# Input projection in wide channel groups with two half sums, and the first norm's squares from channel-major x

## The chip, the core and the metric

The kernel runs on one core of one Trainium2 chip. The metric is device time in microseconds (us): the median of three runs is 1089.92 us (1089.47 to 1090.38). The trace below comes from one more execution, taken with the hardware profiler.

## The reference, cut to what matters

One streaming-encoder layer, 256 tokens, model width 2048, everything in float32:

```
h = rmsnorm(x, norm_mix_g)                 # x is 256 x 2048
a, g, q, k, v = split(h @ w_in)            # 1024 columns each
u = a * sigmoid(g); u = causal_dwconv(u, 31 taps) + b
u = layernorm(u over 1024 channels); conv_out = silu(u)
o = diff_attention(q, k, v, lam)           # 8 heads, 2 x 64 each
mix = concat(conv_out, rmsnorm(o)) @ w_out;  x = x + mix
gate, up = split(rmsnorm(x, norm_ffn_g) @ w_up)    # 2 x 5632
x = x + (gelu(causal_dwconv(gate, 3 taps)) * up) @ w_down
return rmsnorm(x, norm_final_g)
```

## The kernel before, in words

Every large product is built from split operands: a float32 number is held as a high part (rounded to the matmul's type) plus a low part (the rest). Three partial products are summed: high weight x high activation, high weight x low activation, low weight x high activation. Activations live transposed in `xT` (channels on partitions, then chunk k of 128 channels, then high and low side by side, 256 tokens each). Weights stream from memory in pieces of 1 MB (`raw`) over SyncE's queue; ScalarE casts a half piece to `hi` (L151) and VectorE subtracts to get `lo` (L152). One such pair holds four k of a 256-column group. In this document that is a **chunk**. `hi` and `lo` have three buffers each, so the casts can run at most that far ahead of TensorE.

Stages in TensorE's order:

1. While the first weights arrive, 20 small warm-up products (L240) and then the first group of a and of g, k by k (L283). x arrives channel-major (`xt`, two first pieces through ScalarE's queue) and is scaled and split (L113, L114) as it comes. All four accumulator banks of the pool `acc` are in use here.
2. From here TensorE's order is written out by hand (`manual_schedule`). `channel_group` (L202 to L213) computes 256 output channels as two banks, with three matmuls of 256 columns per k and bank (L208, L209, L210). It is called for the groups a1, g1, a2, g2, a3, g3; then `v_slab` computes half of v token-major; then q0, k0, q1, k1, q2, k2, a quarter of v, q3, k3, and the last quarter of v. After each chunk `tick` issues one background step (scores, transposes, values or store of an attention head pair, a step of the layer norm) and two taps of the 31-tap convolution.
3. Layer norm over channels, w_out, then the FFN. The FFN's w_up uses `wide_group` (L179): one matmul of 512 columns with the high weights over the high and the low activations side by side (L187), and one of 256 columns with the low weights (L190), adding into the second half of the bank. The two half sums are added by `halves` (ScalarE copies one half out, VectorE adds the other, L234). w_down is token-major (L218 to L220).
4. The final norm and eight stores.

The norm's factor is applied after the projection: `rb1` holds 1/rms of every token, spread over all partitions, and each a, g and k result is multiplied by it (L375, L383, L531). To get it, x is also loaded token-major in four pieces (`x_sb`), squared and summed on ScalarE (L295), reduced on VectorE (L298), raised to -1/2 on GpSimd (L95, L96), made into two diagonal matrices on VectorE (L102), spread by TensorE (L103) and copied out (L104). The first a and g results are copied out of their banks beforehand (L374, L382), so the banks come free without `rb1`.

On every engine but TensorE a list scheduler sets the order at build time by priority; `prio` shifts a step's priority. A convolution tap is either one VectorE instruction per 128 channels (L350), or ScalarE products (L345) followed by one VectorE add (L346). Scores come out of TensorE, then VectorE adds the mask (L431), ScalarE takes the exponential (L435), VectorE combines the two softmaxes (L445).

Of the kernel before, what the change touches and what calls it, by code (L numbers as in the profile page):

```python
# [27 lines left out]
def block_kernel(  # L28
# [97 lines left out]
    XPARTS = [1, 1, 1, 1, 2, 2, 2, 2, 2, 2]  # L126
    WARM = 10
    SIDE = 2
# [50 lines left out]
    def wide_group(w, c0, xT):  # L179
        ps = [acc.tile([P, 2, T], F32, name="acc") for _ in range(2)]  # L180
        for kc in range(0, KD, 8):
            for k, hi, lo in load(w, kc, 8, c0, GW):
# [17 lines left out]
        return ps  # L200

    def channel_group(w, c0, xT, n_conv=0, ready=None):  # L202
        ps = [acc.tile([P, T], F32, name="acc") for _ in range(2)]
        for kc in range(0, KD, 8):
            for k, hi, lo in ready[kc : kc + 8] if ready else load(w, kc, 8, c0, GW):
                for n in range(2):
                    cs = slice(n * P, (n + 1) * P)
                    nc.tensor.matmul(ps[n], lhsT=hi[:, cs], rhs=xT[:, k, 0, :], start=(k == 0), stop=False)  # L208
                    nc.tensor.matmul(ps[n], lhsT=hi[:, cs], rhs=xT[:, k, 1, :], start=False, stop=False)  # L209
                    nc.tensor.matmul(ps[n], lhsT=lo[:, cs], rhs=xT[:, k, 0, :], start=False, stop=(k == KD - 1))  # L210
                if k % 4 == 3:
                    tick(n_conv)
        return ps  # L213
# [18 lines left out]
    def halves(dst, ps, pool):  # L232
        t1 = pool.tile([P, T], F32, name="half")
        nc.scalar.copy(t1, ps[:, 1, :])  # L234
        nc.vector.tensor_tensor(dst, ps[:, 0, :], t1, op=ALU.add)

    with ph1:
# [5 lines left out]
        ss1 = const.tile([P, NT, D // XW], F32, name="ss1")  # L243
# [10 lines left out]
        for i, nk in enumerate(XPARTS):  # L254
            raw = wraw[k0 * 2 // KD][:, k0 % (KD // 2) : k0 % (KD // 2) + nk, :]
            spans = [(0, GW), (CC, GW)]
            if i < SIDE:
                nc.scalar.dma_start(xraw[:, k0 : k0 + nk, :], xt[:, k0 : k0 + nk, :])
            pieces.append((k0, nk, raw, spans))
            k0 += nk  # L260
        nc.scalar.activation(const.tile([P, 8], F32, name="touch"), mhalf, AF.Copy)
        for i, (k0, nk, raw, spans) in enumerate(pieces):
            if i == 0:
                fetch(mix_g, norm_mix)
# [22 lines left out]
        early = load(wi, 0, 8, GW, GW)  # L287
        for i in range(D // XW):
            if i == 2:
                early.extend(load(wi, 8, 4, GW, GW))  # L290
            cs = slice(i * XW, (i + 1) * XW)
# [4 lines left out]
        early.extend(load(wi, 12, 4, GW, GW))  # L296
# [4 lines left out]
        load_params()  # L301
        with prio(300):
# [64 lines left out]
        for j in range(NP):  # L367
            pa = first[:2] if j == 0 else channel_group(wi, j * GW, xT, n_conv=RATE_A, ready=early if j == 1 else None)
# [8 lines left out]
            pg = first[2:] if j == 0 else channel_group(wi, CC + j * GW, xT, n_conv=RATE_A)  # L377
            for n in range(2):
                g_ = p2.tile([P, T], F32, name="g_")
                if j == 0:  # L380
                    with prio(ATT):
                        nc.vector.tensor_copy(g_, pg[n])  # L382
                nc.vector.tensor_tensor(g_, g_ if j == 0 else pg[n], rb1, op=ALU.mult)  # L383
# [137 lines left out]
        for j in range(H // 2):  # L521
            pq = channel_group(wi, 2 * CC + j * GW, xT, n_conv=RATE_Q)
            qT, kT = [], []
            for n in range(2):
                q_ = p2.tile([P, T], F32, name=f"q{n}")
                nc.scalar.copy(q_, pq[n])
                qT.append(q_)
            pk = channel_group(wi, 2 * CC + H * P + j * GW, xT, n_conv=RATE_Q)
# [76 lines left out]
        bg.extend([seq(ln_total, ln_mean, turn), value, None, ln_var, put, ln_apply])  # L605
# [50 lines left out]
    with ExitStack() as ph2:  # L656
# [10 lines left out]
        for j in range(DFF // GW):  # L667
            pg = wide_group(wu, j * GW, h2T)
            ge = []
            for n in range(2):  # L670
                f = 2 * j + n
                gp = gps[f % 4]
                halves(gp[:, FP:], pg[n], q2)
# [15 lines left out]
            for n in range(2):  # L689
                f = 2 * j + n  # L690
                us = q2.tile([P, T], F32, name="us")
                halves(us, pu[n], q2)
# [12 lines left out]
        STORES = (("dve", 0, 512), ("act", 512, 1024), ("dve", 1024, 1536), ("dve", 1536, 2048))  # L705
# [9 lines left out]
        def finish(t, ss):  # L715
# [4 lines left out]
            c0 = D - XW  # L720
            for eng, lo_, hi_ in STORES:
                xs = x_sb[:, t, lo_:hi_]
                if hi_ == D:
                    nc.vector.scalar_tensor_tensor(xs, xs, r3, gf[:, c0:], op0=ALU.mult, op1=ALU.mult)
                elif eng == "act":
# [119 lines left out]
```

## Time and profile before

| | |
|---|---|
| median of 3 runs | 1089.92 us (1089.47 to 1090.38) |
| the profiled execution's own time | 1090.31 us |
| its span in the trace | 1088.5 us |
| TensorE busy | 1077.5 us (99%) |
| VectorE busy | 764.9 us (70%) |
| ScalarE busy | 599.1 us (55%) |
| GpSimd busy | 15.3 us (1%) |
| DMA | 205.89 MB, mean 189 GB/s |

The busy shares are means over stages that differ: VectorE is busy in nine tenths or more of the slices that hold the convolution and in five to seven tenths later. TensorE's matmuls overlap in the trace (each is shown with its whole duration), so the distance from start to start is the cost of one, not its shown duration. The same holds, by less, on VectorE.

### The profile page before, as it was taken

How to read it: one execution, taken by the hardware profiler on the slowest of the kernel's cores; microseconds unless marked ns; L12 is line 12 of the kernel's file. 1: busy time of each engine (PE TensorE's matmuls, PEld its weight loads, DVE VectorE, ACT ScalarE, POOL GpSimd, SP SyncE). 2: the span in 40 equal slices, each digit the busy share in tenths (PEclk: the TensorE clock that was granted, in tenths of full speed). 3: DMA queues.
4: the chain of work that ended last, by engine and by line, in shares of the span. 5: the costliest groups of instructions: out<-in, count | busy, mean ns of one | idle time of the engine just before them, and what ended most of it. 6: DMA issues, size and time to landing. Idle time of an engine off the chain costs nothing.

```text
span 1088.5 us, 16124 instructions
## 1 busy us (share of the span) xinstructions
PE 1077.5 (99%) x6311; PEld 951.5 (87%) x6311; DVE 764.9 (70%) x1202; ACT 599.1 (55%) x973; POOL 15.3 (1%) x44
## 2 busy tenths in 40 slices
PE   9999999999999999999999999999999999999996
PEld 9999999998888888888888888888888888888885
DVE  6799999988765777776777677776777445454544
ACT  6776889886755454545445444544545434343432
POOL 0000000001000000000000000000000000000000
PEclk9999999999999999999999999999999999999998
DMA  9755544444555555555555555555555655555553
GB/s 352 244 192 185 190 165 152 155 163 148 201 178 178 186 194 192 184 183 181 193 191 193 194 187 180 184 189 189 194 193 190 231 192 196 192 194 193 195 166 107
DMA packets 32844, 205.89 MB, mean 189 GB/s; under 512 B 3712, under 2 KB 4480, under 8 KB 9600
## 3 DMA queue, kind: packets, MB, share of 16 engines
q1 hardware_dynamic: 32336, 203.55, 54.2%
q8 instruction: 49, 0.80, 0.3%
q0 software_dynamic: 144, 1.05, 0.2%
q10 hardware_dynamic: 288, 0.26, 0.1%
q14 instruction: 27, 0.22, 0.1%
HBM read 202.75 MB, written 2.10 MB: 188 GB/s over the span
## 4 chain that ended last, share of the span: by engine, by line
PE 97%; DMA 1%; DVE 1%; ACT 0%; issue 0%; POOL 0%; POOLq 0%; DVEq 0%; SPq 0%; ACTq 0%
PE acc L187 30%; PE acc L190 15%; PE acc L218 11%; PE acc L220 11%; PE acc L219 11%; PE acc L208 5%; PE acc L210 5%; PE acc L209 5%; PE acc L283 2%; DMA v_sb<-in_w_in 1%; PE misc L629 0%; PE misc L426 0%; PE misc L423 0%; PE misc L454 0%; DVE lo L152 0%; ACT hi L151 0%
## 5 line engine op out<-in xcount | busy, mean ns | idle before, releaser
L152 DVE TENSOR_TENSOR lo<-raw,hi 128x1024 fp32r<-128x1024 f32 x368 | 450.0, 1223 | 270.0 <-ACT hi L151 268.7
L151 ACT CAST hi<-raw 128x1024 fp32r<-128x1024 f32 x368 | 386.6, 1051 | 389.3 <-PE acc L220 171.5
L187 PE MATMUL acc<-actT,hi 128*128 128x512 f32 x1408 | 481.7, 395 | 0.0
L190 PE MATMUL acc<-actT,lo 128*128 128x256 f32 x1408 | 368.8, 280 | 0.0
L187 PEld LDWEIGHTS acc<-actT,hi 128*128 128x128 f32 x1408 | 253.3, 188 | 48.5
L190 PEld LDWEIGHTS acc<-actT,lo 128*128 128x128 f32 x1408 | 265.4, 188 | 13.7
L219 PE MATMUL acc<-lo,fT 128*128 128x512 f32 (+1 forms) x355 | 137.5, 387 | 0.0
L220 PE MATMUL acc<-hi,fT 128*128 128x512 f32 (+1 forms) x355 | 137.5, 387 | 0.0
L208 PE MATMUL acc<-actT,hi 128*128 128x256 f32 x448 | 127.6, 285 | 0.0
L210 PE MATMUL acc<-actT,lo 128*128 128x256 f32 x448 | 127.0, 283 | 0.2 <-DVE lo L152 0.2
L209 PE MATMUL acc<-actT,hi 128*128 128x256 f32 x448 | 126.8, 283 | 0.0
L218 PE MATMUL acc<-hi,fT 128*128 128x512 f32 (+1 forms) x355 | 123.8, 387 | 0.0
L208 PEld LDWEIGHTS acc<-actT,hi 128*128 128x128 f32 x448 | 85.9, 192 | 0.7 <-issue 0.7
L210 PEld LDWEIGHTS acc<-actT,lo 128*128 128x128 f32 x448 | 85.9, 192 | 0.4 <-DVE lo L152 0.4
L209 PEld LDWEIGHTS acc<-actT,hi 128*128 128x128 f32 x448 | 85.9, 192 | 0.0
L220 PEld LDWEIGHTS acc<-hi,fT 128*128 128x128 f32 x355 | 66.7, 188 | 13.7
L219 PEld LDWEIGHTS acc<-lo,fT 128*128 128x128 f32 x355 | 66.7, 188 | 13.6
L218 PEld LDWEIGHTS acc<-hi,fT 128*128 128x128 f32 x355 | 66.7, 188 | 13.5
L345 ACT ACTIVATE tap<-u,cols 128x256 f32<-128x256 f32 x160 | 71.0, 503 | 3.7 <-DVE cv L346 2.0
L234 ACT COPY half<-acc 128x256 f32<-128x256 f32 x88 | 32.4, 368 | 56.9 <-PE acc L187 56.9
L346 DVE TENSOR_TENSOR cv<-cv,tap 128x512 f32<-128x512 f32 x80 | 54.7, 685 | 3.0 <-ACT tap L345 1.2
L219 PE MATMUL acc<-lo,mixT 128*128 128x512 f32 x128 | 50.2, 392 | 0.0
(180 smaller groups left out, 913.6 us busy)
## 6 DMA issues: line engine op xcount, KB each, us to landing
raw<-in_w_up SPq DMA_DIRECT2D x88, 1024.0 KB, 4.9
raw<-in_w_down SPq DMA_DIRECT2D x43, 1024.0 KB, 4.9
raw<-in_w_in SPq DMA_DIRECT2D x35, 1024.0 KB, 4.9
raw<-in_w_out SPq DMA_DIRECT2D x14, 1024.0 KB, 4.9
mixT<-in_w_in SPq DMA_DIRECT2D x4, 512.0 KB, 8.4
x_sb<-in_x SPq DMA_DIRECT2D x4, 512.0 KB, 11.0
raw<-in_w_out SPq DMA_DIRECT2D x4, 512.0 KB, 3.5
out<-x_sb SPq DMA_DIRECT2D x8, 256.0 KB, 2.9
```

The lines of the kernel that those rows point to most:

```text
L151: cast(hi, src)
L152: nc.vector.tensor_tensor(lo, src, hi.bitcast(F32), op=ALU.subtract)
L187: nc.tensor.matmul(ps[n], lhsT=hi[:, cs], rhs=xT[:, k], start=(k == 0), stop=last)
L190: nc.tensor.matmul(ps[n][:, 1, :], lhsT=lo[:, cs], rhs=xT[:, k, 0, :], start=False, stop=last)
L208: nc.tensor.matmul(ps[n], lhsT=hi[:, cs], rhs=xT[:, k, 0, :], start=(k == 0), stop=False)
L209: nc.tensor.matmul(ps[n], lhsT=hi[:, cs], rhs=xT[:, k, 1, :], start=False, stop=False)
L210: nc.tensor.matmul(ps[n], lhsT=lo[:, cs], rhs=xT[:, k, 0, :], start=False, stop=(k == KD - 1))
L218: nc.tensor.matmul(ps, lhsT=xT[:, k, 0, ts_], rhs=hi, start=(k == first), stop=False)
L219: nc.tensor.matmul(ps, lhsT=xT[:, k, 0, ts_], rhs=lo, start=False, stop=False)
L220: nc.tensor.matmul(ps, lhsT=xT[:, k, 1, ts_], rhs=hi, start=False, stop=(k == last))
L345: nc.scalar.activation(tmp[:, n, :], upad[c][:, k : k + T], AF.Copy, scale=cwcol(k, c))
L346: nc.vector.tensor_tensor(cv[j], cv[j], tmp, op=ALU.add)
```

## The change

1. `channel_group` is gone; a, g, q and k go through `wide_group` (it gets `n_conv` and `ready`). Per k and bank there are now two matmuls, of 512 and of 256 columns, in the place of three of 256. Results are evacuated by `halves`, now in place: a ScalarE copy (L222) and a VectorE add (L223). For a, g and k the multiplication with `rb1` follows.
2. The sum of squares comes from the channel-major x: ScalarE squares each piece (L260), VectorE adds the pieces up (L263, L282), `token_sums` sums over partitions on TensorE (L109), VectorE copies the result out (L110). Then GpSimd and `spread` as before. The token-major loads of x move into the loop over head pairs.
3. The first a and g results are no longer copied out; the multiplication with `rb1` reads the banks (L361, L371).
4. The first pieces are cut 1,1,1,1,1,1,2,...; 16 warm-up products instead of 20; one x piece instead of two goes through ScalarE's queue, and so does `mix_g`; the first weight piece is first on SyncE's queue.
5. The last attention step and the layer norm are issued in another order.
6. The end: the last sums of squares are taken by one VectorE instruction each, GpSimd only raises the sum to -1/2, and the second half's stores are cut in five over two queues.

Line numbers of L2xx and above differ between the two kernels.

```diff
-    XPARTS = [1, 1, 1, 1, 2, 2, 2, 2, 2, 2]
-    WARM = 10
-    SIDE = 2
+    XPARTS = [1, 1, 1, 1, 1, 1, 2, 2, 2, 2, 2]
+    WARM = 8
+    SIDE = 1
...
-    def wide_group(w, c0, xT):
+    def wide_group(w, c0, xT, n_conv=None, ready=None):
         ps = [acc.tile([P, 2, T], F32, name="acc") for _ in range(2)]
         for kc in range(0, KD, 8):
-            for k, hi, lo in load(w, kc, 8, c0, GW):
+            for k, hi, lo in ready[kc : kc + 8] if ready else load(w, kc, 8, c0, GW):
...
-    def channel_group(w, c0, xT, n_conv=0, ready=None):
-        ps = [acc.tile([P, T], F32, name="acc") for _ in range(2)]
-        for kc in range(0, KD, 8):
-            for k, hi, lo in ready[kc : kc + 8] if ready else load(w, kc, 8, c0, GW):
-                for n in range(2):
-                    cs = slice(n * P, (n + 1) * P)
-                    nc.tensor.matmul(ps[n], lhsT=hi[:, cs], rhs=xT[:, k, 0, :], start=(k == 0), stop=False)
-                    nc.tensor.matmul(ps[n], lhsT=hi[:, cs], rhs=xT[:, k, 1, :], start=False, stop=False)
-                    nc.tensor.matmul(ps[n], lhsT=lo[:, cs], rhs=xT[:, k, 0, :], start=False, stop=(k == KD - 1))
-                if k % 4 == 3:
+                if n_conv is not None and k % 4 == 3:
                     tick(n_conv)
...
-    def halves(dst, ps, pool):
-        t1 = pool.tile([P, T], F32, name="half")
-        nc.scalar.copy(t1, ps[:, 1, :])
-        nc.vector.tensor_tensor(dst, ps[:, 0, :], t1, op=ALU.add)
+    def halves(dst, ps):
+        nc.scalar.copy(dst, ps[:, 1, :])
+        nc.vector.tensor_tensor(dst, ps[:, 0, :], dst, op=ALU.add)
...
+            h0 = k0 % 2
+            sqs = p2.tile([P, 2, T], F32, name="tap") if i > 1 else sq1
+            sq = sqs[:, h0 : h0 + nk, :]
+            nc.scalar.activation(sq, xraw[:, k0 : k0 + nk, :], AF.Square)
+            if i > 1:
+                total = sq1[:, h0 : h0 + nk, :]
+                nc.vector.tensor_tensor(total, total, sq, op=ALU.add)
...
-            fetch(x_sb[:, :, cs], xv[:, :, cs])
-            for t in range(NT):
-                junk = misc.tile([P, 512], F32, name="misc")
-                nc.scalar.activation(junk, x_sb[:, t, cs], AF.Square, accum_out=ss1[:, t, i : i + 1])
         with prio(ATT):
-            nc.vector.tensor_reduce(rstd1, ss1, axis=AX.X, op=ALU.add)
+            nc.vector.tensor_tensor(sq1[:, 0, :], sq1[:, 0, :], sq1[:, 1, :], op=ALU.add)
+            token_sums(rstd1, sq1[:, 0, :])
             rsqrt_of(rstd1, rstd1, D, NORM_EPS, NT)
             spread(rb1, rstd1)
+        early = load(wi, 0, 8, GW, GW)
...
                 if j == 0:
                     with prio(ATT):
-                        nc.scalar.copy(a_, pa[n])
-                nc.vector.tensor_tensor(a_, a_ if j == 0 else pa[n], rb1, op=ALU.mult)
+                        nc.vector.tensor_tensor(a_, pa[n], rb1, op=ALU.mult)
+                else:
+                    halves(a_, pa[n])
+                    nc.vector.tensor_tensor(a_, a_, rb1, op=ALU.mult)
...
         for j in range(H // 2):
+            cs = slice(j * XW, (j + 1) * XW)
+            fetch(x_sb[:, :, cs], xv[:, :, cs])
-            pq = channel_group(wi, 2 * CC + j * GW, xT, n_conv=RATE_Q)
+            pq = wide_group(wi, 2 * CC + j * GW, xT, n_conv=RATE_Q)
...
-                nc.scalar.copy(q_, pq[n])
+                halves(q_, pq[n])
...
-                nc.vector.tensor_tensor(k_, pk[n], rb1, op=ALU.mult)
+                halves(k_, pk[n])
+                nc.vector.tensor_tensor(k_, k_, rb1, op=ALU.mult)
...
-        bg.extend([seq(ln_total, ln_mean, turn), value, None, ln_var, put, ln_apply])
+        bg.extend([turn, seq(ln_total, ln_mean, value), None, None, seq(ln_var, put), ln_apply])
...
+        def last_part(t, ps, cs, before):
+            xs = x_sb[:, t, cs]
+            nc.vector.tensor_tensor(xs, ps, xs, op=ALU.add)
+            sums = const.tile([P, 1], F32, name=f"sums{t}_{cs.start}")
+            junk = misc.tile([P, 512], F32, name="misc")
+            nc.vector.tensor_tensor_reduce(
+                out=junk[:, : cs.stop - cs.start], in0=xs, in1=xs, scale=1.0 / D, scalar=before,
+                op0=ALU.mult, op1=ALU.add, accum_out=sums,
+            )
+            return sums
...
-            for part in ss:
-                nc.gpsimd.tensor_tensor(r3, part, r3, op=ALU.add)
-            nc.gpsimd.tensor_tensor(r3, r3, mhalf[:, 0:1], op=ALU.pow)
+            nc.gpsimd.tensor_tensor(r3, sums, mhalf[:, 0:1], op=ALU.pow)
```

How the built programs' orders stand at the places that matter. **TensorE, end of the first stage.** Before: the last products of the first groups (L283) are followed at once by the second a group (L208 to L210).

```order
L283 MATMUL acc<-actT,hi 128x256 x2
L283 MATMUL acc<-actT,lo 128x256
L208 MATMUL acc<-actT,hi 128x256
L209 MATMUL acc<-actT,hi 128x256
L210 MATMUL acc<-actT,lo 128x256
```

After: between them (L277 is the former L283) stand the norm's partition sums and its spreading. In before L103 stood in the second a group, 74 rows further on.

```order
L109 MATMUL misc<-ones,cv_105 128x1 x2
L103 MATMUL misc<-diag,ones 128x128 x2
L187 MATMUL acc<-actT,hi 128x512
L190 MATMUL acc<-actT,lo 128x256
L187 MATMUL acc<-actT,hi 128x512
```

The two L109 and the two L103 have moved ahead of all of the second a group.

**VectorE, the same place.** In before, the diagonals (L102), the copy of the spread factor (L104) and the first four multiplications (L375, L383) read tiles in SBUF that L374 and L382 had filled:

```order
L102 TENSOR_SCALAR diag<-ident,rstd_106 128x128 x2
L152 TENSOR_TENSOR lo<-raw,hi 128x1024
L315 TENSOR_SCALAR nrq_467<-rstd_106 128x2
L307 TENSOR_REDUCE ls<-lamp 128x2
L310 TENSOR_TENSOR nlam<-ls 128x1
L104 COPY rb_108<-misc 128x256
L311 TENSOR_SCALAR nlam<-nlam 128x1
L375 TENSOR_TENSOR a_487<-a_487,rb_108 128x256
```

In the change the same chain begins with the copy of the sums (L110), and a `lo` subtraction stands ahead of the diagonals; the multiplications read the banks (`acc`):

```order
L110 COPY rstd_104<-misc 128x2
L298 TENSOR_SCALAR nlam<-nlam 128x1
L152 TENSOR_TENSOR lo<-raw,hi 128x1024
L102 TENSOR_SCALAR diag<-ident,rstd_104 128x128 x2
L302 TENSOR_SCALAR nrq_482<-rstd_104 128x2
L104 COPY rb_106<-misc 128x256
L361 TENSOR_TENSOR a_502<-acc,rb_106 128x256
L361 TENSOR_TENSOR a_504<-acc,rb_106 128x256
```

So the multiplications that free the banks have come ahead, and their inputs are now the banks themselves.

**VectorE, during the attention of the third head pair.** Before, all that stands between one `lo` and the next, with the mask step of the scores (L431), two of the softmax's small steps and two convolution adds (L346):

```order
L431 ISA pr,mx<-misc,mask,nrq_467 128x128
L431 ISA mx 128x1
L431 ISA pr,mx<-misc,mask,nrq_467 128x256
L431 ISA mx 128x1
L346 TENSOR_TENSOR cv_475<-cv_475,tap 128x512
L431 ISA pr,mx<-misc,mask,nrq_467 128x128
L431 ISA mx 128x1
L431 ISA pr,mx<-misc,mask,nrq_467 128x256
L431 ISA mx 128x1
L443 RECIPROCAL r_2284<-sm 128x2
L439 RECIPROCAL sm<-sm 128x2
L346 TENSOR_TENSOR cv_475<-cv_475,tap 128x512
```

After, in the second head pair's attention, the last twelve rows of the 31 between two `lo` subtractions (the mask step is L422, its combination L436; the convolution's L346 and L350 are L333 and L337; `cv_490` and `cv_491` are the third and the fourth pair of channel blocks):

```order
L333 TENSOR_TENSOR cv_490<-cv_490,tap 128x512
L436 SCALAR_TENSOR_TENSOR pr<-pr,sm 128x128
L436 SCALAR_TENSOR_TENSOR pr<-pr,sm 128x256
L337 SCALAR_TENSOR_TENSOR cv_490<-u_496,cols,cv_490 128x256 x2
L430 RECIPROCAL sm<-sm 128x2
L333 TENSOR_TENSOR cv_491<-cv_491,tap 128x512
L333 TENSOR_TENSOR cv_490<-cv_490,tap 128x512
L431 SCALAR_TENSOR_TENSOR sm<-sm,nlam 128x2
L337 SCALAR_TENSOR_TENSOR cv_491<-u_498,cols,cv_491 128x256 x2
L436 SCALAR_TENSOR_TENSOR pr<-pr,sm 128x128
L436 SCALAR_TENSOR_TENSOR pr<-pr,sm 128x256
L333 TENSOR_TENSOR cv_491<-cv_491,tap 128x512
```

The convolution has moved forward: the whole of it stands ahead of the last q's evacuation in VectorE's order, and 31 rows stand between these two `lo` subtractions where the stretch shown of before has 12.

## Rows read from the trace of the kernel before

**Rows 1.** The page: busy time of each engine, and the chain that ended last.

```profile
PE 1077.5 (99%) x6311; PEld 951.5 (87%) x6311; DVE 764.9 (70%) x1202; ACT 599.1 (55%) x973; POOL 15.3 (1%) x44
PE 97%; DMA 1%; DVE 1%; ACT 0%; issue 0%; POOL 0%; POOLq 0%; DVEq 0%; SPq 0%; ACTq 0%
```

**Rows 2.** Windows: stretch, length, busy of PE, PEld, DVE, ACT, POOL; clock, DMA.

```profile
30.00:60.00 30.00, 29.76 (x249) 29.55 (x247) 24.36 (x48) 22.27 (x43) 0.94 (x2) 1.00 0.65 219
...
150.61:214.06 63.45, 63.45 (x535) 62.21 (x534) 61.19 (x145) 58.58 (x152) 4.11 (x6) 1.00 0.44 150
```

**Rows 3.** Timeline: start, us, line; subtractions and first matmuls of two chunks.

```profile
149.39 1.22 DVE L152 TENSOR_TENSOR lo<-raw,hi 128x1024 fp32r<-128x1024 f32 x1
155.21 0.28 PE L208 MATMUL acc<-actT,hi 128*128 128x256 f32 x1
212.84 1.22 DVE L152 TENSOR_TENSOR lo<-raw,hi 128x1024 fp32r<-128x1024 f32 x1
215.65 0.28 PE L208 MATMUL acc<-actT,hi 128*128 128x256 f32 x1
```

**Rows 4.** Timeline, TensorE, channel groups: start, us, engine, line, operation.

```profile
65.40 0.28 PE L208 MATMUL acc<-actT,hi 128*128 128x256 f32 x1
...
88.44 0.28 PE L208 MATMUL acc<-actT,hi 128*128 128x256 f32 x1
```

**Rows 5.** Windows, L187 alone, FFN: length, busy of PE and PEld (count), clock.

```profile
400.00:800.00 400.00, 391.05 (x1145) 205.61 (x1145) 1.00 0.55 189
```

**Rows 6.** Timeline, TensorE: the first matmul after the first stage.

```profile
29.91 0.28 PE L208 MATMUL acc<-actT,hi 128*128 128x256 f32 x1
```

**Rows 7.** Timeline, layer norm's sum over partitions and its power.

```profile
265.89 0.50 PE L109 MATMUL misc<-ones,part 128*128 128x1 f32 x4
266.43 0.16 DVE L110 COPY rln<-misc 128x2 f32<-128x2 f32 x1 [0.71 <-PE misc L109]
266.68 0.19 POOL L95 TENSOR_SCALAR rln<-rln 128x2 f32<-128x2 f32 x1 [2.10 <-DVE rln L110]
266.95 0.70 POOL L96 TENSOR_TENSOR rln<-rln,mhalf 128x2 f32<-128x2 f32 x1
```

**Rows 8.** Timeline, VectorE: the first norm's diagonals, and a subtraction behind them.

```profile
35.54 0.48 DVE L102 TENSOR_SCALAR diag<-ident,rstd 128x128 f32<-128x128 f32 x2 [0.89 <-POOL rstd L96]
35.94 1.22 DVE L152 TENSOR_TENSOR lo<-raw,hi 128x1024 fp32r<-128x1024 f32 x1
```

**Rows 9.** Lines, VectorE and ScalarE, 150.61 to 214.06: count | busy, mean ns | idle.

```profile
L346 DVE TENSOR_TENSOR cv<-cv,tap 128x512 f32<-128x512 f32 x25 | 17.1, 685 | 0.7 <-ACT tap L345 0.2
L350 DVE SCALAR_TENSOR_TENSOR cv<-u,cols,cv 128x256 f32<-128x256 f32 x24 | 10.5, 478 | 0.1
L431 DVE CUSTOM_DVE_ANT_0 pr<-misc,mask,nrq 128x256 f32<-128x256 f32 x11 | 5.3, 481 | 0.0
L431 DVE CUSTOM_DVE_ANT_0 pr<-misc,mask,nrq 128x128 f32<-128x128 f32 x11 | 3.8, 347 | 0.1
L531 DVE TENSOR_TENSOR k<-acc,rb 128x256 f32<-128x256 f32 x4 | 1.5, 413 | 0.0
...
L345 ACT ACTIVATE tap<-u,cols 128x256 f32<-128x256 f32 x48 | 21.4, 505 | 0.6 <-DVE cv L346 0.6
```

**Rows 10.** Timeline, TensorE at the layer norm's mean.

```profile
255.13 0.70 PE L560 MATMUL misc<-part,onesc 128*128 128x256 f32 x2 [0.69 <-DVE part L555]
```

**Rows 11.** Timeline, the start: warm-up products and the first real matmuls.

```profile
0.98 4.64 PE L240 MATMUL misc<-ones 128*128 128x128 f32 x20 [0.98 <-POOL ones L86]
5.27 2.01 PE L283 MATMUL acc<-actT,hi 128*128 128x256 f32 x8
7.59 1.12 PE L283 MATMUL acc<-actT,hi 128*128 128x256 f32 x8
```

**Rows 12.** Timeline, the end: the last square, and GpSimd's power.

```profile
1080.67 0.39 ACT L710 ACTIVATE misc<-x_sb 128x256 f32<-128x256 f32 x1 [0.35 <-DVE x_sb L708]
1081.59 0.55 POOL L719 TENSOR_TENSOR rstd<-rstd,mhalf 128x1 f32<-128x1 f32 x1
```

More of the change, by code (lines that the diff above doesn't have):

```diff
@@ L258, in block_kernel @@
                 nc.scalar.dma_start(xraw[:, k0 : k0 + nk, :], xt[:, k0 : k0 + nk, :])
+                nc.scalar.dma_start(mix_g, norm_mix)
             pieces.append((k0, nk, raw, spans))
@@ L367, in block_kernel @@
         for j in range(NP):
-            pa = first[:2] if j == 0 else channel_group(wi, j * GW, xT, n_conv=RATE_A, ready=early if j == 1 else None)
+            pa = first[:2] if j == 0 else wide_group(wi, j * GW, xT, n_conv=RATE_A, ready=early if j == 1 else None)
             an, gn = [], []
@@ L381, in block_kernel @@
                     with prio(ATT):
-                        nc.vector.tensor_copy(g_, pg[n])
-                nc.vector.tensor_tensor(g_, g_ if j == 0 else pg[n], rb1, op=ALU.mult)
+                        nc.vector.tensor_tensor(g_, pg[n], rb1, op=ALU.mult)
+                else:
+                    halves(g_, pg[n])
+                    nc.vector.tensor_tensor(g_, g_, rb1, op=ALU.mult)
                 gn.append(g_)
@@ L672, in block_kernel @@
                 gp = gps[f % 4]
-                halves(gp[:, FP:], pg[n], q2)
+                halves(gp[:, FP:], pg[n])
                 nc.vector.tensor_tensor(gp[:, FP:], gp[:, FP:], rb2, op=ALU.mult)
@@ L691, in block_kernel @@
                 us = q2.tile([P, T], F32, name="us")
-                halves(us, pu[n], q2)
+                halves(us, pu[n])
                 nc.vector.tensor_tensor(us, us, ge[n], op=ALU.mult)
@@ L704, in block_kernel @@
         CUT = 3
-        STORES = (("dve", 0, 512), ("act", 512, 1024), ("dve", 1024, 1536), ("dve", 1536, 2048))
+        STORES = {
+            0: ((nc.vector, nc.sync, 512), (nc.scalar, nc.sync, 512), (nc.vector, nc.sync, 512), (nc.vector, nc.sync, 512)),
+            1: (
+                (nc.vector, nc.sync, 256), (nc.scalar, nc.scalar, 384), (nc.vector, nc.sync, 512),
+                (nc.vector, nc.sync, 448), (nc.vector, nc.scalar, 448),
+            ),
+        }
         def residual(t, ps, cs, out_ss):
@@ L713, in residual, with finish @@
             )
-        def finish(t, ss):
-            r3 = rstd3[:, t : t + 1]
-            for part in ss:
-                nc.gpsimd.tensor_tensor(r3, part, r3, op=ALU.add)
-            nc.gpsimd.tensor_tensor(r3, r3, mhalf[:, 0:1], op=ALU.pow)
[L720 to L725, printed above, removed]
-                    nc.scalar.activation(xs, xs, AF.Copy, scale=r3)
-                else:
-                    nc.vector.tensor_scalar_mul(xs, xs, r3)
-                nc.sync.dma_start(ov[:, t, lo_:hi_], xs)
+        def last_part(t, ps, cs, before):
[8 more added lines that the diff above has]
+            return sums
+        def finish(t, sums, cs):
+            r3 = rstd3[:, t : t + 1]
+            nc.gpsimd.tensor_tensor(r3, sums, mhalf[:, 0:1], op=ALU.pow)
+            lo_ = 0
+            for eng, queue, width in STORES[t]:
+                xs = x_sb[:, t, lo_ : lo_ + width]
+                cut = min(max(cs.start - lo_, 0), width)
+                if cut < width:
+                    xg = xs[:, cut:]
+                    nc.vector.scalar_tensor_tensor(xg, xg, r3, gf[:, lo_ + cut : lo_ + width], op0=ALU.mult, op1=ALU.mult)
+                if not cut:
+                    pass
+                elif eng is nc.scalar:
+                    nc.scalar.activation(xs[:, :cut], xs[:, :cut], AF.Copy, scale=r3)
+                else:
+                    nc.vector.tensor_scalar_mul(xs[:, :cut], xs[:, :cut], r3)
+                queue.dma_start(ov[:, t, lo_ : lo_ + width], xs)
+                lo_ += width
         def plain_end(s, pd):
@@ L754, in block_kernel @@
             token_step(pd[0], rest, 0, fT, 0, NF - 1)
-            residual(0, pd[0], slice(c0, D), ss3[:, 0, s : s + 1])
-            finish(0, [ss3[:, 0, s : s + 1]])
+            whole = slice(c0, D)
+            finish(0, last_part(0, pd[0], whole, rstd3[:, 0:1]), whole)
             token_step(pd[1], rest[:-CUT], 1, fT, 0, NF - 1)
-            ss4 = const.tile([P, 2], F32, name="ss4")
             hw = XW // 2
```

24 lines of the change are left out of this document (9 added, 15 removed).

## The prediction

> **What bounds the kernel now.** I read the page first: TensorE is busy 1077.5 of 1088.5 us and is 97% of the chain that ended last [rows 1]. So the time is TensorE's stream of matmuls plus its few gaps. A change gains by a shorter stream, and loses wherever another engine comes late. VectorE's mean of 70% says little, so I read the windows stage by stage. From 150.61 to 214.06 us, where convolution and attention run beside the q and k groups, VectorE is busy 61.19 of 63.45 us and ScalarE 58.58, while TensorE has no gap [rows 2]. There VectorE is within 4% of being the bound. Last I read in the timeline how far ahead it is: the `lo` subtraction that ends at 150.61 belongs to a chunk whose first matmul starts at 155.21; the one that ends at 214.06 to a chunk that starts at 215.65 [rows 3]. The lead is 4.6 us at one end and 1.6 at the other. VectorE already loses 3.0 us of lead in this stretch; its end saves it.
>
> **1. Two matmuls in the place of three.** In the channel groups 192 matmuls start in 88.44 - 65.40 = 23.04 us, 0.120 each, 0.360 per three [rows 4]. In the FFN the pair of 512 and 256 columns is already there: 1145 of the L187 were recorded in 400 us [rows 5], 0.3494 per pair. The gain is 0.0106 us. There are 14 groups (a and g three times, q and k four) with 32 pairs each, 448 in all: 4.7 us. I take 4.6, 0.0103 a pair.
>
> The Trainium skill ("TensorE: Matmul & The Clock Gate", Back-to-back issue gap) gives columns/2.4 ns plus 2.5 ns for an isolated matmul: one fixed cost fewer, 2.5 ns per pair, 1.1 us in all as an estimate. By that the sum below would be 3.5 us higher. The rows differ from it by a factor of four, and they decide.
>
> **2. Evacuation by halves.** 28 VectorE adds more (two each in six a and g groups and eight q and k groups) and 20 ScalarE copies more. Ahead of the attention VectorE has idle time for them, 5.6 of 30 us [rows 2]; in the attention it has not. They are counted there, in 4.
>
> **3. The first norm's factor.** In before TensorE goes on at 29.91 [rows 6], since the first results were copied out of their banks. Now the four banks come free only by multiplications that need `rb1`, and TensorE itself stands behind L109 and L103. The chain from the end E of the first stage, by rows of the same instructions: from L109 to L110 0.54 (four products there, two here; I take 0.45), to GpSimd 0.25, to its power 0.27, the power 0.70 [rows 7]: E + 1.7. By then VectorE stands at a `lo` subtraction ahead of the diagonals. Its cast needs a `hi` buffer that TensorE releases at E; with the cast of some 1 us before it, the subtraction of 1.22 [rows 8] ends at E + 2.2. Then two diagonals, 0.40 from their start to the next start [rows 8], L103 and its way to the copy some 0.45, the copy and a multiplication at 0.41 each (L531, [rows 9]): E + 3.9. In before there is 0.24 of visible idle time from 30 to 60 us [rows 2]; with what the modelled ends hide I call it 0.4. Cost 3.5. Without the subtraction in between it is 3.0, with further waits of small steps 4.5. All of TensorE's stream is queued behind this wait; the casts may go on in it, but only three buffers deep.
>
> **4. VectorE in the attention.** I compare the stretch between the same two chunks, by the programs' order. Before, it holds 18 `lo`, 25 L346, 24 L350, 11 mask steps of each width, 4 multiplications of k, which are the counts of [rows 9]. After, it holds 18 `lo`, 32 adds of the convolution (7 more), 32 of its other taps (8 more), 12 mask steps of each width with their combination (1 more), and 8 adds of halves. At the means of [rows 9]: 7 x 0.685 + 8 x 0.478 + 8 x 0.413 + 2 x (0.481 + 0.347) = 13.6 us. Neighbours overlap by 0.08 (two diagonals of 0.48 together leave the engine after 0.40 [rows 8]); for 27 instructions that is 2.2. So 11.4 more, 72.6 us.
>
> TensorE needs for its stretch 215.65 - 155.21 = 60.4 [rows 3], less 14 chunks of channel groups with 8 pairs of 0.0103 each, 1.15: 59.3. VectorE has 13.3 too much. It starts with a lead of at most 4.6, if it is as good as before: 8.7 stays as TensorE's waiting. With VectorE's own idle time of 2.3 us, waits on ScalarE [rows 2], 11.0. The work also comes in lumps: 31 rows between two subtractions, by the same means some 11 us against one chunk of TensorE's. I take 10. The lower end is 0, if VectorE arrives with a larger lead than rows show; the upper 13. ScalarE has 4 copies and 14 tap products more at 0.45 (21.4 for 48 [rows 9]): 58.6 + 8 = 66.6, late too, inside the same wait.
>
> Behind the stretch VectorE has less to do than before, since the convolution is through. TensorE's wait of 0.69 for the last sums of the convolution at the layer norm's mean [rows 10], with some 0.2 beside it, goes: -0.9. What is late next there is nothing that the rows show.
>
> **5. Start.** The first real matmul stands at 5.27 [rows 11] and the first stage ends at 29.91. The weights come first on their queue, and pieces are smaller. ScalarE has the squares on top, and TensorE's 12 matmuls per k take 1.44 by [rows 4]; scaling, cast and squares of one k come to about 1.4, only just hidden. I take -0.5, between -1.5 and +1.5.
>
> **6. End.** After the last VectorE add, ScalarE's square starts at 1080.67 and GpSimd's power at 1081.59 [rows 12], with GpSimd's add between. One VectorE instruction (0.48 [rows 9]) replaces square and add: -0.3 to -0.6, with the new cut of the stores inside it. I take -0.4.
>
> **The sum.** -4.6 + 3.5 + 10 - 0.9 - 0.5 - 0.4 = +7.1 on the profiled execution's own 1090.31: 1097.4. That is 0.4 above the median of the runs shown, so I predict 1097.0.
>
> **Rivals.** *VectorE catches up between the lumps.* The lump of 11 us costs only what exceeds one chunk's time with scores and transposes (about 4.5) and a lead of 4.6, so 1.9, if VectorE is at full lead before each; two smaller lumps of some 8 us then cost nothing. Sum: -4.6 + 3.5 + 1.9 - 0.9 - 0.5 - 0.4 = -1.0, so 1088.9. For it: TensorE had no gap with VectorE 96% busy. Against: the sum over the stretch, which no order of the work changes.
>
> *TensorE stays the bound throughout* (the other side). The shorter matmuls are the whole effect, and VectorE's adds find room. Without 4's wait the sum is -2.9, so 1087.0; with half the wait of 3 as well, 1085.3. It decides from the point where VectorE's stretch takes under 63.9 us (59.3 + 4.6), so if the added instructions cost under 2.7. Against: 2.3 us of idle time is all there is [rows 2].
>
> *The clock falls in the waits.* The clock granted to TensorE reads 1.00 in all windows [rows 2, 5], its 2.4 GHz level; TensorE had no gap near 4 us in them, so no row shows a fall. Its price is in the rows of the start: the first eight L283 took 2.01 us, a later eight 1.12 [rows 11]; if everything from 0.98 to 7.1 us ran at half the rate, 3 us were lost. One fall after the first stage gives 1100, falls in two lumps of VectorE's too 1106. The skill, on the page named above under HAM oscillation, says that gaps of waiting between groups of matmuls put the engine back to its lower clock, each time anew. No row here bears that out or excludes it.
>
> **Chances.** Forecast (VectorE the bound in the attention) 0.60, its own range 1093 to 1102; caught up between lumps 0.13, 1087.7 to 1092; TensorE the bound 0.17, 1084 to 1087.7; clock 0.10, 1100 to 1107. The range 1086 to 1103 leaves out about two in ten. A measurement here can tell 0.2%, 2.2 us, from no change: faster 0.17, same 0.13, slower 0.70.
>
> **What would show it.** Right: gaps of TensorE that end with a `lo` from VectorE between some 155 and 225 us, 10 us together; one gap near 4 us behind the first stage; pairs at 0.349 us in the q groups; no gap at the mean; VectorE without idle time through the stretch. Wrong: TensorE without gaps there (then step 4 fails, in lead or in durations), a granted clock under 1.00 behind a gap, or a first stage that ends after 31.

## The result, and the profile after

The changed kernel takes 1103.7 us (median of 4 runs, 1102.23 to 1105.1) against 1090.05 before: ratio 1.0128, 95% interval 1.0115 to 1.0140. It is slower by 13.7 us, about twice the forecast, and outside the range. The profiled execution took 1102.23 us, 11.9 more than that of before; its span is 1100.2 us. It is the fastest of the four: what the others took beyond it (1.3 to 2.9 us) stands in no trace.

The page first: busy times, and the chain that ended last. They answer to [rows 1].

```profile
PE 1079.7 (98%) x5863; PEld 931.1 (85%) x5863; DVE 781.1 (71%) x1248; ACT 603.2 (55%) x981; POOL 14.6 (1%) x41
PE 94%; DVE 2%; ACT 1%; issue 1%; DMA 1%; POOL 0%; SPq 0%; POOLq 0%; DVEq 0%; ACTq 0%
```

TensorE does less (448 matmul instructions fewer), yet is busy longer, and 6% of the chain now lie elsewhere. Shorter work that is busy longer points to the clock. What TensorE waits for (line, releaser: total us, times, longest):

```profile
PE misc L414 <- DVE k L525: 5.9, 3, 3.1
PE misc L103 <- DVE diag L102: 2.2, 1, 2.2
PE acc L187 <- DVE a L361: 1.1, 1, 1.1
...
PE misc L109 <- DVE part L568: 0.8, 1, 0.8
```

L414 is the scores' product, L525 the multiplication of k by `rb1`: the large wait is not for a `lo`. The wait at the layer norm's mean [rows 10] is gone, but one of the same size stands at its variance (L109).

**Behind the first stage.** Timeline of TensorE (start, us, line), where before had its next matmul at once [rows 6]:

```profile
29.08 0.50 PE L109 MATMUL misc<-ones,cv 128*128 128x1 f32 x4
31.76 1.22 PE L103 MATMUL misc<-diag,ones 128*128 128x128 f32 x4 [2.18 <-DVE diag L102]
34.04 0.77 PE L187 MATMUL acc<-actT,hi 128*128 128x512 f32 x1 [1.06 <-DVE a L361]
...
36.74 0.63 PE L187 MATMUL acc<-actT,hi 128*128 128x512 f32 x1
...
37.38 0.63 PE L187 MATMUL acc<-actT,hi 128*128 128x512 f32 x1
...
38.00 0.39 PE L187 MATMUL acc<-actT,hi 128*128 128x512 f32 x1
...
38.35 0.39 PE L187 MATMUL acc<-actT,hi 128*128 128x512 f32 x1
```

From the end of the first stage to the first pair it is 34.04 - 29.08 = 5.0 us (forecast: 3.9). Then the pairs come at 0.64 us until 37.4 and at 0.35 from 38.0. The windows give the granted clock there (stretch, length, busy, clock, DMA):

```profile
30.00:34.00 4.00, 1.22 (x4) 0.64 0.74 264
34.00:38.00 4.00, 3.96 (x12) 0.50 0.03 6
38.00:42.00 4.00, 4.00 (x25) 1.00 0.00 0
```

0.50 is the lower of the two levels, 1.2 GHz. Between 34.04 and 38.00 six pairs stand where eleven would fit: 1.9 us lost besides the wait.

**At the scores of the second head pair.** VectorE's timeline, with no idle time in it:

```profile
176.18 0.42 DVE L223 TENSOR_TENSOR k<-acc,k 128x256 f32<-128x256 f32 x1
176.53 0.68 DVE L333 TENSOR_TENSOR cv<-cv,tap 128x512 f32<-128x512 f32 x1
177.12 0.42 DVE L525 TENSOR_TENSOR k<-k,rb 128x256 f32<-128x256 f32 x1
177.46 1.22 DVE L152 TENSOR_TENSOR lo<-raw,hi 128x1024 fp32r<-128x1024 f32 x1
178.59 0.42 DVE L223 TENSOR_TENSOR k<-acc,k 128x256 f32<-128x256 f32 x1
178.93 0.68 DVE L333 TENSOR_TENSOR cv<-cv,tap 128x512 f32<-128x512 f32 x1
...
180.20 1.22 DVE L152 TENSOR_TENSOR lo<-raw,hi 128x1024 fp32r<-128x1024 f32 x1
181.34 0.42 DVE L525 TENSOR_TENSOR k<-k,rb 128x256 f32<-128x256 f32 x1
```

The second k's add ends at 179.0. Its multiplication starts at 181.34, since a convolution add, the first head's mask steps and a `lo` stand between them in the queue. ScalarE's copy is not what is late: the second k's ends at 177.4. TensorE, which had finished its matmuls and the first head's scores by 178.8, waits:

```profile
178.16 0.61 PE L417 MATMUL misc<-k,q 64*128 64x256 f32 x4
181.90 0.80 PE L414 MATMUL misc<-k,q 64*128 64x128 f32 x4 [3.14 <-DVE k L525]
```

The clock falls here too, and behind the third pair's wait of 2.2 us:

```profile
175.00:180.00 5.00, 3.76 (x25) 1.00 0.62 210
180.00:185.00 5.00, 3.10 (x13) 0.63 0.50 172
185.00:190.00 5.00, 5.00 (x24) 0.69 0.09 38
...
210.00:215.00 5.00, 2.61 (x24) 1.00 0.38 159
215.00:220.00 5.00, 5.00 (x30) 0.66 0.60 210
```

**Where the 11.7 us of span went**, by the starts of the same steps in the two timelines (after less before):

| step | difference there | made up of |
|---|---|---|
| end of the first stage | -0.8 | start |
| first v slab | +3.6 | +4.0 wait (5.0 less 1.0 that L103 and a short stop take in before), +1.9 clock, -1.5 pairs |
| first scores | +3.1 | -0.5 pairs |
| second pair's store, behind the third pair's scores | +12.8 | +7.1 at the scores (5.9 of it waits; 0.7 the second pair's products at the lower clock), +3.5 clock behind them, -0.9 pairs |
| last v slab | +12.2 | -0.6 pairs |
| behind the layer norm, and start of the FFN | +12.2 | 0 |
| end | +11.7 | -0.5 end |

In sum: waits 11.1, clock 5.4, pairs -3.5, start -0.8, end -0.5. Outside the span the changed kernel takes 2.0 us, before 1.8, so 0.2 of the end's gain comes back there.

### The profile page after: what moved, and what is told of

Read it like the earlier page. It is cut to its first block, busy times and chain, and to the rows that moved or that the text cites. A ratio compares the mean times of both kernels' runs of the same rounds, so it can differ in the third digit from the quotient of the medians.

```text
span 1100.2 us, 15303 instructions
## 1 busy us (share of the span) xinstructions
PE 1079.7 (98%) x5863; PEld 931.1 (85%) x5863; DVE 781.1 (71%) x1248; ACT 603.2 (55%) x981; POOL 14.6 (1%) x41
## 4 chain that ended last, share of the span: by engine, by line
PE 94%; DVE 2%; ACT 1%; issue 1%; DMA 1%; POOL 0%; SPq 0%; POOLq 0%; DVEq 0%; ACTq 0%
PE acc L187 39%; PE acc L190 20%; PE acc L207 11%; PE acc L208 11%; PE acc L209 11%; PE acc L277 1%; DVE lo L152 1%; DMA v_sb<-in_w_in 0%; ACT hi L151 0%; PE misc L623 0%; DMA mixT<-in_xt 0%; DVE cv L333 0%; PE misc L445 0%; ACT tap L332 0%; PE misc L417 0%
## 5 line engine op out<-in xcount | busy, mean ns | idle before, releaser
L187 PE MATMUL acc<-actT,hi 128*128 128x512 f32 x1856 | 643.8, 398 | 1.1 <-DVE a L361 1.1
L187 PEld LDWEIGHTS acc<-actT,hi 128*128 128x128 f32 x1856 | 338.6, 189 | 70.2 <-issue 2.3
L208 PE MATMUL acc<-lo,fT 128*128 128x512 f32 (+1 forms) x355 | 137.5, 387 | 0.0
L209 PEld LDWEIGHTS acc<-hi,fT 128*128 128x128 f32 x355 | 66.7, 188 | 13.7
L207 PEld LDWEIGHTS acc<-hi,fT 128*128 128x128 f32 x355 | 66.7, 188 | 13.7
L208 PEld LDWEIGHTS acc<-lo,fT 128*128 128x128 f32 x355 | 66.6, 188 | 13.6
L333 DVE TENSOR_TENSOR cv<-cv,tap 128x512 f32<-128x512 f32 x80 | 54.5, 684 | 2.0 <-ACT tap L332 0.4
L208 PE MATMUL acc<-lo,mixT 128*128 128x512 f32 x128 | 50.2, 392 | 0.0
L209 PE MATMUL acc<-hi,mixT 128*128 128x512 f32 x128 | 49.9, 390 | 0.0
L207 PE MATMUL acc<-hi,mixT 128*128 128x512 f32 x128 | 48.6, 393 | 0.0
L337 DVE SCALAR_TENSOR_TENSOR cv<-u,cols,cv 128x256 f32<-128x256 f32 x80 | 35.1, 478 | 0.4
L222 ACT COPY gp<-acc 128x256 f32<-128x256 f32 x44 | 16.3, 369 | 32.6 <-PE acc L187 32.6
L207 PE MATMUL acc<-hi,actT 128*128 128x256 f32 (+1 forms) x96 | 31.5, 328 | 0.0
L208 PE MATMUL acc<-lo,actT 128*128 128x256 f32 (+1 forms) x96 | 31.3, 326 | 0.0
L209 PE MATMUL acc<-hi,actT 128*128 128x256 f32 (+1 forms) x96 | 31.2, 325 | 0.0
```

The lines of the kernel that those rows point to most:

```text
L187: nc.tensor.matmul(ps[n], lhsT=hi[:, cs], rhs=xT[:, k], start=(k == 0), stop=last)
L207: nc.tensor.matmul(ps, lhsT=xT[:, k, 0, ts_], rhs=hi, start=(k == first), stop=False)
L208: nc.tensor.matmul(ps, lhsT=xT[:, k, 0, ts_], rhs=lo, start=False, stop=False)
L209: nc.tensor.matmul(ps, lhsT=xT[:, k, 1, ts_], rhs=hi, start=False, stop=(k == last))
L222: nc.scalar.copy(dst, ps[:, 1, :])
L333: nc.vector.tensor_tensor(cv[j], cv[j], tmp, op=ALU.add)
```

## The experiments

Theory A is the prediction's step 4: VectorE has too much work beside the attention. Theory B came out of the trace: the result that the scores need goes through copy, add and multiplication on two busy queues, and what stands between these steps makes TensorE wait. A third point is the clock. Each run's before is the one measured beside it, 1089.35 to 1089.54 us. "The changed kernel" is at 1103.7, beside a before of 1090.05; differences to it are uncertain by the 0.5 to 0.7 us between the befores.

**e1: the first results copied out.** In the changed kernel:

```diff
-                        nc.vector.tensor_tensor(a_, pa[n], rb1, op=ALU.mult)
+                        nc.scalar.copy(a_, pa[n])          # g: nc.vector.tensor_copy
...
-                    nc.vector.tensor_tensor(a_, a_, rb1, op=ALU.mult)
+                nc.vector.tensor_tensor(a_, a_, rb1, op=ALU.mult)
```

> The changed kernel, but with the first a and g results copied out of their banks first (ScalarE for a, VectorE for g), as in before; the multiplication with rb1 comes afterwards. TensorE's spreading products then stand 36 rows into the second a group instead of ahead of it. Theory (the wait behind the first stage comes from banks that need rb1, and the clock falls in it): the wait of 2.2 and 1.1 us and the 1.7 us lost at half clock between 34 and 38 go, 5 to 6.5 us less than the changed kernel's 1103.7, about 1098; granted clock 1.00 from 30 to 60. Rival (the wait only moves to the lo subtraction or to L103): 0 to 2 us less, 1102, with a new wait of TensorE of 2 us or more between 29 and 42.

1098.01 us, 5.7 less than the changed kernel; ratio to before 1.0078 (1.0063 to 1.0093). TensorE's window, answering to 0.64 and 0.50 above:

```profile
30.00:60.00 30.00, 30.00 (x177) 1.00 0.51 176
```

No wait and no fall. The cause of the first loss is shown: banks that need `rb1`. The waits at the scores stay (6.9 us, 5.9 before this edit).

**e2: k's evacuation urgent.**

```diff
+                with prio(ATT):
                     halves(k_, pk[n])
                     nc.vector.tensor_tensor(k_, k_, rb1, op=ALU.mult)
```

> The changed kernel, but the evacuation of k (copy, add, multiplication) has the scheduler's urgent priority: the same instructions, and the last multiplication of k stands behind one lo subtraction less on VectorE. Theory A (step 4 of the prediction: VectorE has too much work in the stretch): the waits at the scores become waits for lo; 0 to 2 us less than 1103.7, 1102 to 1104. Theory B (only the order and latency of the chain copy, add, multiplication makes TensorE wait at the scores): the waits of 0.5, 3.1 and 2.2 us at L414 shrink to under 1 us together, and the clock stays at 1.00 from 150 to 240: 8 to 9 us less, 1095.

1099.98 us (ratio 1.0097, 1.0082 to 1.0112), 3.7 less. Between the two. TensorE's waits:

```profile
PE misc L414 <- DVE k L526: 3.7, 3, 2.2
...
PE acc L190 <- DVE lo L152: 0.4, 1, 0.4
```

The same instructions in another order give 2.2 us of waits back at the scores, and what A expected, waits for `lo`, is 0.4. B's 1095 is not reached either: a `lo` still stands ahead of the second k's multiplication, and the third pair waits 2.2 us as before.

**e3: k by three matmuls.** k goes through the old `channel_group` and one multiplication straight from the bank:

```diff
-                halves(k_, pk[n])
-                nc.vector.tensor_tensor(k_, k_, rb1, op=ALU.mult)
+                nc.vector.tensor_tensor(k_, pk[n], rb1, op=ALU.mult)
```

> The changed kernel, but k (not a, g, q) by three matmuls of 256 columns as in before, evacuated by one VectorE multiplication: 8 adds and 8 ScalarE copies fewer. Theory A (work): 6 adds of 0.34 us less in the stretch, so 2 us less wait, and 0.8 us more matmul time in 128 groups of three: 1 to 3 us less than 1103.7, about 1102. Theory B (latency of the chain): the waits at the scores go to under 1 us, the clock stays at 1.00: 8 us less, 1096.

1095.0 us (ratio 1.0056, 1.0039 to 1.0073), 8.7 less. TensorE's waits and the clock in the attention:

```profile
PE misc L103 <- DVE diag L102: 2.2, 1, 2.2
PE misc L458 <- DVE pr L449: 1.8, 1, 1.8
```

```profile
170.00:190.00 20.00, 20.00 (x140) 1.00 0.39 141
190.00:215.00 25.00, 23.17 (x195) 1.00 0.50 173
```

The waits at the scores are gone, though only 2.7 us of VectorE's work went (8 adds), with 8 copies on ScalarE. That fits B; the edit takes the chain and this work away together, so it does not part them by itself. One wait of 1.8 us came in their place, at the transposes, behind q's adds; the clock stayed at 1.00 through it.

**e4: 16 convolution taps left out.**

```diff
-            for k in range(CONV_K):
+            for k in range(CONV_K if j < 2 else CONV_K - 8):
```

> The changed kernel with 23 instead of 31 convolution taps for the last two of four channel pairs (the last 8 taps of each are left out of the computation): 16 taps fewer, some 10 us of VectorE work and 8 us of ScalarE work. VectorE's order up to the second head pair's scores is nearly as in the changed kernel; the convolution ends before the third pair's. Theory A (work): the third pair's wait of 2.2 us and its half clock of 1.5 us go, and waits for lo behind them too; second pair's stays: 4 us less than 1103.7, about 1099.5. Theory B (latency): VectorE's chain for k is shorter where no convolution stands between, so the same 4 us at the third pair; but if the wait at the third pair stays above 1 us with the convolution gone, B alone is right.

1104.24 us (ratio 1.0133, 1.0117 to 1.0148): no gain from some 10 us less work. VectorE at the third pair, where the convolution has ended:

```profile
209.22 0.42 DVE L223 TENSOR_TENSOR k<-acc,k 128x256 f32<-128x256 f32 x1
209.55 0.68 DVE L348 TENSOR_TENSOR tap<-tap,cv 128x512 f32<-128x512 f32 x1
210.15 1.22 DVE L152 TENSOR_TENSOR lo<-raw,hi 128x1024 fp32r<-128x1024 f32 x1
...
211.96 0.42 DVE L525 TENSOR_TENSOR k<-k,rb 128x256 f32<-128x256 f32 x1
```

```profile
PE misc L414 <- DVE k L525: 7.4, 5, 3.4
```

The wait there was 2.2 us and is 3.4. The layer norm's first sums (L348), a `lo` and the mask steps stand between k's two steps now. VectorE still has no idle time up to these scores; its idle time comes behind them (20.3 of 25 us busy from 200 to 225). So e4 shows that what stands between the steps can be any work, and that the work taken away does not come to TensorE's good. It does not show what an emptier VectorE would do.

**e5: pairs for a and g alone, in the kernel before.** All else as before.

```diff
-            pa = first[:2] if j == 0 else channel_group(wi, j * GW, xT, n_conv=RATE_A, ready=early if j == 1 else None)
+            pa = first[:2] if j == 0 else wide_group(wi, j * GW, xT, n_conv=RATE_A, ready=early if j == 1 else None)
...
+                else:
+                    half_sums(a_, pa[n])     # copy and add, as the new halves; g alike
```

> The kernel before with one part of the change alone: a and g (not q, k) by pairs of 512 and 256 columns, evacuated by halves; the first norm, the start, the attention and the end as in before. Term 1 alone: 192 pairs at 0.0106 us less, 2.0 us less than before's 1089.5, so 1087.5 (1087.0 to 1088.0), if the 12 more VectorE adds lie in idle time. Rival (any VectorE work more shows at the attention): 1089.5 or more.

1095.26 us (ratio 1.0053, 1.0041 to 1.0066): slower, against the expectation. Up to the last scores TensorE is 2.1 us ahead of before (240.7 against 242.8): 0.6 from a first stage that ended earlier in this execution, 1.4 from the pairs (68.6 us from there to the first v slab, 70.1 in before) where term 1 has 2.0. Then:

```profile
PE misc L570 <- DVE part L565: 5.5, 1, 5.5
```

```profile
258.00:260.00 2.00, 2.00 (x9) 0.50 0.06 23
```

The layer norm's mean waits for the last sums of the convolution, 5.5 us instead of 0.7 [rows 10]. VectorE has them ready 2.7 us later than before (257.7 against 255.1; the 12 adds are some 4 us of its work), and TensorE arrives 2.1 earlier. Behind this wait too the clock is at half, which costs another 1.5 us up to the variance.

**e6: products in the first wait.** In the changed kernel, behind `token_sums`:

```diff
+            idle = misc.tile([P, 512], F32, name="misc")
+            for _ in range(10):
+                nc.tensor.matmul(idle[:, :P], lhsT=ones, rhs=ones, start=True, stop=True)
```

> The changed kernel with ten more 128-column products of ones (as the warm-up's), which TensorE does between the norm's partition sums and its spreading, in the wait behind the first stage; nothing uses their result. Theory (the wait itself costs 3.3 us and the clock's fall 2 us more): the clock stays at 1.00 from 30 to 42 and the first pairs of the second a group come at 0.35 us, 1.5 to 2 us less than the changed kernel there (TensorE at 100 us earlier by that much against the end of the first stage). Rival (the fall depends on nothing that such products change): the same half clock up to 38.

```profile
32.00:34.00 2.00, 0.93 (x7) 1.00 0.37 152
34.00:36.00 2.00, 2.00 (x13) 1.00 0.02 8
```

The clock stays at 1.00, and from the end of the first stage to the first v slab it takes 72.3 us instead of 74.4: the fall cost 2.1 us there. The whole run took 1108.82 us (ratio 1.0178, 1.0163 to 1.0194), 5.1 more than the changed kernel: TensorE comes earlier to the scores, VectorE's order there came out another way, and the waits at the scores are 10.7 us. The gain is given back and more.

**e7 and e8: both repairs.** e7 is e1 and e3 together; e8 has q by three matmuls too.

> The changed kernel with both of the first experiments that helped: the first a and g results copied out first, and k by three matmuls. If the two causes are separate, their gains add: 5.7 and 8.7 less than 1103.7, 1089.3. If they share a cause (VectorE's work as a whole), less: 1092 or more.

> The same, and q by three matmuls too: only a and g are left in pairs. 8 adds and 8 copies fewer; 128 groups of three cost 0.7 us more. Chain theory (what TensorE waits for is a result that goes through several instructions on busy queues): the 1.8 us wait at the transposes of the third run, behind q's adds, goes as well: 1088. Work theory: 1089 or more, since nothing but 2.7 us of VectorE work that fits in goes.

e7: 1088.89 us (ratio 0.9997, 0.9988 to 1.0006); e8: 1088.95 (0.9995, 0.9986 to 1.0003). The two gains add: 5.7 + 8.7 = 14.4, expected 1089.3. Both kernels are level with before. In e8 no wait over 0.2 us is left from the end of the first stage on, and it is no faster than e7, which still has 1.4 at the transposes; e8's two expectations (1088, and 1089 or more) lie too close to be told apart by 1088.95.

**e9 and e10: the kernel before with a and g in pairs, the new layer norm's order and the new end;** e10 has q in pairs too.

```diff
-        bg.extend([seq(ln_total, ln_mean, turn), value, None, ln_var, put, ln_apply])
+        bg.extend([turn, seq(ln_total, ln_mean, value), None, None, seq(ln_var, put), ln_apply])
```

> The kernel before with three parts of the change: a and g in pairs, the new order of the layer norm's steps, and the new end. The 5.5 us wait that e5 had at the layer norm's mean is bridged, if the mean stands one background step later behind the scores' transposes: then 2.0 less from the pairs and 0.5 from the end, 1087.0 (1086.5 to 1087.5), under both kernels. Rival (VectorE's added work has to be paid somewhere before the layer norm is through): a wait of 2 us or more at the layer norm and 1089 or more.

> The same with q in pairs as well, evacuated by a copy and an add; k stays with three matmuls. 128 pairs at 0.005 less, 0.7 us. Theory B (a chain of several instructions right ahead of the scores is what hurts, and q has a whole group's time): no wait at the scores, 1086.5. Theory A (VectorE's work in the stretch): waits at the scores, the transposes or the layer norm that exceed the gain, 1088 or more.

e9: 1093.02 us (ratio 1.0032, 1.0021 to 1.0043); e10: 1090.28 (1.0006, 0.9997 to 1.0015). Both came out as their rivals had it: VectorE's added work is paid. e9 still waits at the mean:

```profile
PE misc L570 <- DVE part L565: 3.7, 1, 3.7
```

So the order of the layer norm is worth some 2 us here, not the whole wait. e8, with the same adds for a and g, waits 0.2 at the mean. It differs in the first norm (squares from channel-major x) and in the cut of the first pieces. Its `rb1` comes earlier (37.6 against 38.4 us), VectorE begins the convolution at 43.2 instead of 45.0, and has the last sums ready at 256.9 instead of 259.1. No run parts the norm from the pieces.

e10 has no wait at the scores, as B expected, but waits 2.5 us at the transposes, and the clock falls there:

```profile
PE misc L464 <- DVE pr L455: 2.5, 2, 1.6
```

```profile
162.00:164.00 2.00, 2.00 (x12) 0.54 0.20 74
```

At the mean it doesn't wait, though its VectorE is no earlier than e9's (last sums at 259.6): its TensorE comes there at 259.7, where e9's came at 255.5.

**e11 and e12: a and g multiplied on GpSimd.** e11 is e7, e12 is e1, both with

```diff
-                nc.vector.tensor_tensor(a_, a_, rb1, op=ALU.mult)
+                (nc.vector if j == 0 else nc.gpsimd).tensor_tensor(a_, a_, rb1, op=ALU.mult)   # g alike
```

> e7 (first results copied out, k by three matmuls) with the 12 multiplications of a and g (three groups) by rb1 on GpSimd, which is idle there, in the place of VectorE: 4 us of VectorE work less before the attention, the same results. Work theory: e7's waits of 1.4 us at the transposes and 0.8 at the layer norm's variance shrink: 1087.0 to 1088.0 against e7's 1088.9 and before's 1089.5. Rival (GpSimd is slow, its reads slow VectorE, or the start's spread decides): 1088.9 or more.

> e1 (first results copied out, q and k in pairs as in the change) with the 12 multiplications of a and g on GpSimd: VectorE has 4 us less to do before the attention, while the chain of k (copy, add, multiplication) and what stands between its steps stay. Theory A (work): e1's waits of 6.9 us at the scores shrink by 4 us, and the clock's falls with them: 1092 against e1's 1098.0. Theory B (order): the waits at the scores stay at 5 to 8 us: 1097 to 1099.

e11: 1086.73 us (ratio 0.9978, 0.9969 to 0.9988), 0.2% faster than before. The waits at the transposes are gone, as the work theory had it: there, work counts. The 0.8 at the variance stays. GpSimd needs 0.9 to 2.3 us for each (VectorE 0.41 [rows 9]), which nobody waits for:

```profile
L377 POOL TENSOR_TENSOR a<-a,rb 128x256 f32<-128x256 f32 x6 | 8.5, 1433 | 29.4 <-DVE a L236 29.4
```

e12: 1096.34 us (1.0060, 1.0044 to 1.0076), 1.7 less than e1, though its interval overlaps e1's and the two profiled executions took the same (1098.6 and 1098.68). The waits at the scores are unchanged in sum:

```profile
PE misc L414 <- DVE k L525: 6.9, 3, 2.9
```

4 us less work move the waits at the scores by nothing, as B has it; A's 1092 is far off, B's 1097 to 1099 is missed by 0.7.

## Why the prediction was wrong

The direction was right: the kernel is slower, and the time is lost beside the attention and in the wait for `rb1` behind the first stage. The size and part of the mechanism were wrong, in these steps.

- **"The clock falls in the waits"** is the step that failed most. It was a rival with 0.10, beside the forecast, though each of the forecast's own waits invites it. It came with every one of the three large waits: 1.9 + 3.5 = 5.4 us. Its price per fall was too high (3 us, 1.5 to 2 measured). It belonged in the sum: 1097.4 + 5.4 is 1102.8, against 1102.2 profiled. That this comes so close is luck: the other terms miss by 2.5 us upwards (pairs, step 3, layer norm) and 3.3 downwards (step 4, start, end). e1 and e6 show the fall's cause for the first wait: without the gap, or with products in it, 1.00.
- **Step 4** had the place and not far from the size (10 forecast; the scores took 7.1 longer, 5.9 of it waits), but the wrong mechanism, so the size was luck. It was worked out as an excess of work that ends in waits for `lo`; there is none of them in the list. VectorE is as full there as forecast, but it was so before (busy 86.2 of 90 us from 150 to 240, 85.7 before). TensorE waits for k, whose three steps stand apart in VectorE's queue. e12 takes work away without effect on these waits, e2 shortens them by order alone, e3 takes the chain away and they go. The prediction counted "8 adds of halves" as work and didn't ask what stands behind each on its own queue.
- The work itself does count, but elsewhere: at the layer norm's mean in e5 and e9, at the transposes in e10, and between e7 and e11.
- **Step 3**: 5.0 us against 3.9 for the chain. L103 took 1.22 us at the lower clock (0.6 at the upper, in the layer norm), and its copy and the multiplication came that much later. Net 4.0 for 3.5, since before loses 1.0 there and not 0.4.
- **Term 1**: 3.5 of 4.6 us. The pairs come at 0.353, beside the attention (first two lines) and in the a and g groups (last two, 32 pairs apart), not at the FFN's 0.349:

```profile
155.70 0.40 PE L187 MATMUL acc<-actT,hi 128*128 128x512 f32 x1
...
157.11 0.40 PE L187 MATMUL acc<-actT,hi 128*128 128x512 f32 x1
...
57.26 0.40 PE L187 MATMUL acc<-actT,hi 128*128 128x512 f32 x1
...
68.56 0.40 PE L187 MATMUL acc<-actT,hi 128*128 128x512 f32 x1
```

Four pairs in 1.41 us and 32 in 11.30, (0.352 each over the 186 from 38.00 to the first v slab), where the three of before kept 0.360. The Trainium skill's fixed cost ("TensorE: Matmul & The Clock Gate", Back-to-back issue gap) would have given 1.1, as an estimate; the 3.5 measured lies nearer to the rows.
- **The layer norm**: -0.9 forecast, 0 measured. The wait at the mean went and one of 0.8 at the variance came. "What is late next there is nothing that the rows show" was wrong.
- **Start** -0.8 for -0.5: not shown. The last matmul of the first stage stands between 28.5 and 30.7 us in the ten profiled executions with the new start, between 29.0 and 29.8 in the four with the old one. The hit is luck.
- **End** -0.5 for -0.4: right. Its reason was not: the power starts 2.19 us after the last matmul's start (2.22 before), so square and add gave nothing. The rest, with the stores, gave the half microsecond:

```profile
1093.16 0.48 DVE L720 CUSTOM_DVE_ANT_0 misc<-x_sb,sums 128x256 f32<-128x256 f32 x1
...
1093.78 0.56 POOL L728 TENSOR_TENSOR rstd<-sums,mhalf 128x1 f32<-128x1 f32 x1 [3.85 <-DVE sums L720]
```

The last square's VectorE instruction stands behind a multiplication that had been put ahead of it.

Open: which rule of the scheduler put the steps of k so far apart, why e6's order came out worse, and how much of e3's gain the 8 adds would give without the chain.

## What to carry to other kernels

A forecast that contains waits of TensorE of 2 us and more has to contain what the clock costs behind them: add it to the sum, not to the rivals (1.5 to 2 us each here). When an evacuation grows from one instruction to three, ask what stands between the three on their queues and who waits for the last, before adding up their durations; the result that is needed soonest keeps the short chain. A gain of a microsecond on the bound engine is only worth it if the next engine has that microsecond: here it took an idle engine's help (e11) to keep it.

## What the runs showed of the hardware

- The granted clock fell to 0.50 in or behind each of the 18 single waits of TensorE over 2.1 us in the profiled executions (the changed kernel's three among them), for some 3 to 7 us each time. Below that the runs draw no line: behind e3's wait of 1.8 and before's of 0.7 it read 1.00, behind e10's of 1.6 it read 0.54.
- A pair of matmuls took 0.353 us in the a and g groups and beside the attention, 0.349 in the FFN of before [rows 5], with the clock at 1.00 in all three.
- GpSimd multiplied 128x256 in 0.9 to 2.3 us beside a busy VectorE (e11, e12).
